# A hybrid decoder layer on one core: GpSimd's sums, dots, folds and three weight remainders on VectorE, and gate products placed behind their operands

## The chip, the core and the metric

The kernel runs on one core of one Trainium2 chip. A core has five engines that run their own queues in order and wait for each other through semaphores: TensorE (PE: matmuls from on-chip memory, SBUF, into the accumulation memory, PSUM), VectorE (DVE: elementwise work and scans), ScalarE (ACT: activation functions, casts, copies), GpSimd (POOL: elementwise work, and transfers that it issues itself) and SyncE (SP: here it only issues transfers). PEld is TensorE's loading of stationary operands. The metric is the time of one execution in microseconds of device time; lower is better. A profile is one execution with every instruction recorded.

## The reference

One layer, batch 1, 1024 tokens, 1024 channels. All arithmetic is to float32 accuracy.

```python
mod = silu(c) @ mod_w + mod_b
shift, scale, gate = split(mod, 3)
h = rmsnorm(x, norm_g) * (1 + scale) + shift
cv, cg, cs, lx, ls = split(h @ w_in, 5)              # 1024 columns each

v = causal_depthwise_conv(cv * sigmoid(cg), dw_w, dw_b)      # 31 taps
v = silu(layernorm(v, cln_g, cln_b))                         # over channels
y_conv = (v @ pw2_w + pw2_b) * silu(cs)

xs = causal_depthwise_conv(lx, sc_w, sc_b)                   # 4 taps
r = sigmoid(xs @ wr + br); i = sigmoid(xs @ wi + bi)         # by heads of 128
a = exp(-8 * r * softplus(-lam))
hs = linear_scan(a, sqrt(1 - a*a) * i * xs)                  # h_t = a_t h_{t-1} + b_t
y_lru = hs * silu(ls)

x = x + (1 + gate) * (concat(y_conv, y_lru) @ w_out)
out = rmsnorm(x, final_g)
```

## The kernel before

Everything is held transposed: channels on the 128 partitions, tokens along the free axis, so a tensor of 1024 channels is eight tiles of 128x1024. A float32 product is made of three reduced-precision ones: each operand is split into a high part (a cast, on ScalarE) and a remainder (full minus high, a subtraction of two SBUF tiles), and high x high, high x remainder and remainder x high are accumulated. The suffixes `hi` and `lo` (weights), `h` and `l` (inputs) name these parts.

**The slots.** The 40 output tiles of `w_in` and the eight of the LRU half of `w_out` are worked off one after the other; each is a slot with a number `n` (0 to 47) and takes 48 matmuls of 128x512: eight input tiles, two halves of the tokens, three products. Slots 0 to 6 are a start group. `ORDER` (line 35) lists the others: `i25` is output tile 25 of `w_in`, `g1` stands for the gate products of LRU head 1. `weights` (468) prepares a slot's weights: a transfer into `raw`, a cast to `whi` on ScalarE, and the remainder `wlo` on GpSimd for slots below `EARLY` and on VectorE from there on. `raw`, `whi` and `wlo` have two buffers each. Slots 4 to 13 have theirs on GpSimd before.

**The LRU half.** When a slot of `lx` is done, `evac_in` (1112) reads it from PSUM: two activations on ScalarE, six tap accumulations on VectorE make `xs`; `split` makes `xsh` on ScalarE and `xsl` (`xs` minus `xsh`, VectorE). `gates` (1156) then has 12 matmuls of 128x512: the gate weights' high part with `xsh`, the same with `xsl`, their remainder with `xsh`. Sigmoids, exponential, tangent and square root follow on ScalarE, products and the scan on VectorE, and at last `yh` and `yl`, the inputs of the LRU half of `w_out` (slots 40 to 47).

**The convolution.** `conv_tile` (1003) has 31 taps for each of the eight tiles of `v`. Five tiles are accumulated tap by tap on VectorE; the three in `POOLED` (1, 3, 5) by ScalarE, which writes scaled copies `cq` and `co`, and by transfers that GpSimd issues and that add them into `es` and `oo` (`conv_pooled`, 1054). At the end of a pooled tile, `last` (1082) folds `es` and `oo` into the tile `c` with three instructions on the engine `FOLD`. `conv_sum` (1090) adds up the eight finished tiles in the order `SUMS`: seven additions of 128x1024, six on GpSimd and the last on VectorE. All but the last may start only when the first matmul of slot `CSUM` has started (`after`). The layer norm (1196) takes the mean from that sum, by one product with ones (`mean`, line 1202). Its result goes through the pointwise product (`pw2`), while PE works on the LRU half of `w_out`.

**The gate modulation.** `gate_mod` (1186) is called in slots 14 to 21 (`GM`). It loads 128 rows of `mod_w` into `modw` through SP and calls `dot` (794), which multiplies them with the activated `c` (in `sc`) and sums along the row. Where `GDOT` is `'POOL'`, GpSimd makes the product and ScalarE sums it in an activation with an accumulator; where it is `'DVE'`, VectorE does both in one instruction. The sixteen dots of shift and scale at the start already run on VectorE.

**The order.** All instructions go first into a `Plan` (102). `order` (159) simulates the engines with costs for every operation and writes each engine's queue in the planned order; the chip then runs the queues in this order, with waits on real data. A free engine takes the ready operation with the lowest `prio`: a slot's work has about its number, the convolution has 1000 and more, so it fills what is left. `ready` is the planned end of what an operation needs, plus a latency (line 201). The planner lets VectorE and GpSimd wait for each other where both work on SBUF alone (`lock`, `held`).

Of the kernel before, what the change touches and what calls it, by code (L numbers as in the profile page):

```python
# [12 lines left out]
ALU = mybir.AluOpType  # L13
# [34 lines left out]
TLATE = 2  # L48
QGATES = ((2, 5), (3, 0), (3, 2), (3, 2))
PEARLY = (3,)  # L50
CSUM = 36
OUT_A, OUT_P, OUT_Z = (6,), (0, 1, 2), (7,)
KORD = (0, 1, 2, 3, 4, 5, 6, 7)
WPW = ("DVE", "DVE", "DVE", "DVE")
# [12 lines left out]
SPP = 25  # L67
PAD = 16
GLO = 'DVE'
GDOT = 'POOL'  # L70
FOLD = 'POOL'
EARLY = 14
ISSUE, FLIGHT, RATE = 1.0, 10.0, 3.0
GM = 14
TAPP = 15
# [20 lines left out]

class Op:
    __slots__ = ("eng", "cost", "emit", "prio", "table", "bufs", "succ", "wait", "ready",
                 "seq", "reserve", "columns", "lock", "end", "psum", "lag")


class Plan:
# [21 lines left out]
                    yield (it, i)  # L124

    def op(self, eng, cost, emit, prio, r=(), w=(), table=None, after=(), reserve=0,
           columns=0, lock=False, lag=0.0):
        o = Op()
        o.lag = lag
        o.eng, o.cost, o.emit, o.prio, o.table = eng, cost, emit, prio, table  # L130
        o.succ, o.ready, o.seq, o.reserve = [], 0.0, len(self.ops), reserve
        o.columns = columns
        o.lock = not lag and eng == "POOL" or eng == "DVE" and lock
        r, w = list(self.keys(r)), list(self.keys(w))
        preds = set(after)
        for k in r:
            if k in self.writer:
                preds.add(self.writer[k])
        for k in w:
            if k in self.writer:  # L140
                preds.add(self.writer[k])
            preds.update(self.readers.get(k, ()))
        for k in r:
            self.readers.setdefault(k, []).append(o)
        for k in w:
            self.writer[k] = o
            self.readers[k] = []
        preds.discard(o)
        o.wait = len(preds)
        for p in preds:  # L150
            p.succ.append(o)
        o.bufs = list(dict.fromkeys(k[0] for k in r + w if isinstance(k[0], Buf)))
        for b in o.bufs:
            b.left += 1
        o.psum = [(b, any(k[0] is b for k in w)) for b in o.bufs if b.pool == "bank"]
        self.ops.append(o)
        return o

    def order(self):
        free = {p: cap for p, (_, _, _, cap) in self.pools.items()}  # L160
        live = set()
        engines = ("PE", "ACT", "DVE", "POOL", "SP")
        until = {"PE": 1.0, "ACT": 2.5, "DVE": 2.6, "POOL": 1.1, "SP": SP0}
        pending = {e: [] for e in engines}
        for o in self.ops:
            if o.wait == 0:
                pending[o.eng].append(o)
        releases, out, table, t, ticks = [], [], "silu", 0.0, {0: self.BUSY}
        held = {"DVE": 0.0, "POOL": 0.0}
        waiting = None  # L170
        left = len(self.ops)

        def clear(o):

            return max((e + self.LATENCY[g] for b, w in o.psum
                        for d in ((b.read, b.written) if w else (b.written,))
                        for g, e in d.items() if g != o.eng), default=0.0)

        def done(o, end):
            until[o.eng] = end  # L180
            if o.lag:
                self.pipe = max(self.pipe, end) + o.lag
                end = max(self.pipe, end + FLIGHT)
            elif o.eng == "SP":
                self.pipe = end = max(self.pipe, end - o.cost) + o.cost
                until["SP"] = max(end - o.cost + 0.4, end - BACKLOG)
            o.end = end
            for b, w in o.psum:
                (b.written if w else b.read)[o.eng] = end
            for b in o.bufs:  # L190
                b.left -= 1
                if b.left == 0 and b.pool in free:
                    heapq.heappush(releases, (end, b.name, b.pool))
            for s in o.succ:
                lat = 0.0 if o.eng == "PE" and s.eng == "PE" else \
                    0.11 if o.eng == s.eng == "DVE" else self.LATENCY[o.eng]
                if o.eng == "SP" and o.prio > 0:
                    lat = LANDING if o.prio < 37 else 3.0
                if s.prio >= 1000 and s.eng != o.eng and o.prio < 2000:
                    lat += MARGIN  # L200
                s.ready = max(s.ready, end + lat)
                s.wait -= 1
                if s.wait == 0:
                    pending[s.eng].append(s)

        while left:
            while releases and releases[0][0] <= t:
                free[heapq.heappop(releases)[2]] += 1
            moved, later = False, []
            if waiting and held["DVE"] <= t + 1e-9:  # L210
                o, waiting, moved = waiting, None, True
                held["POOL"] = t + o.cost
                done(o, t + o.cost)
            for e in engines:
                if until[e] > t + 1e-9:
                    continue
                best, key = None, None
                for o in pending[e]:
                    if o.ready > t + 1e-9:
                        continue  # L220
                    if e == "DVE" and o.lock and held["POOL"] > t + 1e-9:
                        later.append(held["POOL"])
                        continue
                    k = (o.prio + (2.0 if o.table and o.table != table else 0.0), o.seq)
                    if key is not None and k >= key:
                        continue
                    need = {}
                    for b in o.bufs:
                        if b.pool in free and b not in live:
                            need[b.pool] = need.get(b.pool, o.reserve * (b.pool == "big")) + 1  # L230
                    if any(free[p] < n for p, n in need.items()):
                        continue
                    if o.psum and clear(o) > t + 1e-9:
                        later.append(clear(o))
                        continue
                    best, key = o, k
                if best is None:
                    continue
                o, moved = best, True
                pending[e].remove(o)  # L240
                left -= 1
                cost = o.cost
                if o.table and o.table != table:
                    cost, table = cost + self.SWITCH, o.table
                if e == "PE":
                    if t < self.COLD or ticks.get(int(t / self.TICK) - 1, 0) < self.BUSY:
                        cost *= 2
                    i = int((t + cost) / self.TICK)
                    ticks[i] = ticks.get(i, 0) + o.columns
                end = t + cost  # L250
                out.append((t, o))
                for b in o.bufs:
                    if b.pool in free and b not in live:
                        live.add(b)
                        free[b.pool] -= 1
                if e == "POOL" and o.lock and held["DVE"] > t + 1e-9:
                    waiting, until[e] = o, float("inf")
                    continue
                if o.lock:
                    if e == "DVE":  # L260
                        end = max(t, held["POOL"]) + cost
                    held[e] = end
                done(o, end)
            if not moved:
                nxt = later + [u for u in until.values() if t + 1e-9 < u < float("inf")]
                nxt += [o.ready for e in engines for o in pending[e] if o.ready > t + 1e-9]
                if releases:
                    nxt.append(releases[0][0])
                assert nxt, "no operation can go on"
                t = min(nxt)  # L270
        return out
# [11 lines left out]
def hymba_layer(ctx: ExitStack, tc: tile.TileContext, xT, vecs, mod_w, w_first, w_in,  # L283
# [806 lines left out]
    def conv_sum():  # L1090
        for i in SUMS[1:]:
            a, end = c[SUMS[0]] if i == SUMS[1] else csum, i == SUMS[-1]
            TT(1000 + 5 * i, "DVE" if end else "POOL", csum, a, c[i], ALU.add, r=[a, c[i]],
               w=[csum], after=[] if end else [started[CSUM]])


# [59 lines left out]
    def gates(i, n):  # L1156
# [3 lines left out]
        for j, (dst, b) in enumerate(((r, "br"), (g, "bi"))):  # L1160
            ps = Two(f"gate{i}_{j}")
            for c0, c1 in FULL:
                def emit(j=j, ps=part(ps, c0, c1), c0=c0, c1=c1):
                    for lhs, rhs, st in ((hi, xh, 0), (hi, xl, 1), (lo, xh, 2)):
                        pe.matmul(ps(), lhs()[:, j, :], rhs()[:, c0:c1], start=st == 0,
                                  stop=st == 2)
                S.op("PE", 3 * 0.2267, emit, n + 0.01 * j, [hi, lo, xh, xl], halves(ps, c0, c1),
                     columns=3 * H)
                ACT(n + 0.2, part(dst, c0, c1), part(ps, c0, c1), AF.Sigmoid, H, bias=vec(b, i),
                    r=halves(ps, c0, c1), w=[dst])  # L1170
        pr = n + 1.0
# [314 lines left out]
```

## Time and profile before

| | us |
|---|---|
| three runs | 753.58, 750.99, 749.26 |
| median | 750.99 |
| the profiled execution, its time | 752.39 |
| the profiled execution, its span from first to last instruction | 750.5 |

The busy times of the engines and the stretches that matter are shown where the prediction uses them. In rows of instructions, `out<-in` are tile names of the program; a time in brackets at the end is the idle time of the engine ahead of that instruction, with what ended it. `L480` are the slots' matmuls, `L1165` the gate products, `L352` a tensor-tensor operation of VectorE or GpSimd, `L344` a scalar-tensor-tensor operation of VectorE, `L333` and `L325` ScalarE's activations and casts. Matmuls overlap, so the distance between two starts, not the duration of one, is what a matmul costs.

PE's work in order: the start group to about 85 us, the slots of `w_in` with the gate products to 481.85 us, the LRU half of `w_out` to 574 us, `pw2` to 651 us, the convolution half of `w_out` to 740 us, and the last stores.

### The profile page before, as it was taken

The numbers are of one execution on the slowest core, as the hardware profiler recorded it, in microseconds if no ns is written. First come the engines' busy times: TensorE is split into PE (matmuls) and PEld (weight loads), VectorE is DVE, ScalarE is ACT, GpSimd is POOL, SyncE is SP. The second block draws the span as 40 slices with busy tenths as digits, with TensorE's granted clock in tenths as the row PEclk, the third lists the DMA queues.
The fourth block names the chain that finished last, engine by engine and source line by source line (L and its number), as shares of the span: only waits on it lengthen the run. The fifth ranks groups of instructions, "written<-read, shape, count | busy, mean of one in ns | idle before, by whom it ended". The sixth has DMA issues, their size and how long they took to land. (4 is left out here: it accounts for less than half of the span.)

```text
span 750.5 us, 8997 instructions
## 1 busy us (share of the span) xinstructions
PE 732.9 (98%) x3314; PEld 608.0 (81%) x3314; DVE 619.9 (83%) x858; ACT 466.0 (62%) x627; POOL 162.0 (22%) x137
## 2 busy tenths in 40 slices
PE   9999999999999999999999899999999999999994
PEld 8888888887888888888888688878888888878884
DVE  6999999999799881788899995839799857998544
ACT  7660697677978977855959486714584334656331
POOL 0033023363163331532113343020000000000003
PEclk9999999999999999999999899999999999999998
DMA  9961034686699799598383436643224330534006
GB/s 338 408 210 50 0 117 102 154 182 155 173 220 221 144 216 218 123 216 176 103 177 73 108 69 195 168 166 143 99 98 155 116 123 17 208 113 141 28 1 224
DMA packets 37052, 111.59 MB, mean 149 GB/s; under 512 B 4112, under 2 KB 12816, under 8 KB 37008
## 3 DMA queue, kind: packets, MB, share of 16 engines
q1 hardware_dynamic: 23616, 75.97, 29.0%
q0 software_dynamic: 12528, 34.26, 25.2%
q10 hardware_dynamic: 864, 0.79, 0.3%
q8 instruction: 26, 0.43, 0.2%
q14 instruction: 18, 0.15, 0.1%
HBM read 64.16 MB, written 12.58 MB: 102 GB/s over the span
## 5 line engine op out<-in xcount | busy, mean ns | idle before, releaser
L480 PE MATMUL ps<-uh,whi 128*128 128x512 f32 x576 | 224.6, 390 | 0.0
L480 PE MATMUL ps<-ul,whi 128*128 128x512 f32 x576 | 224.5, 390 | 0.0
L480 PE MATMUL ps<-uh,wlo 128*128 128x512 f32 x576 | 224.4, 390 | 0.0
L480 PEld LDWEIGHTS ps<-uh,whi 128*128 128x128 f32 x576 | 108.5, 188 | 22.6
L480 PEld LDWEIGHTS ps<-ul,whi 128*128 128x128 f32 x576 | 108.3, 188 | 22.5
L480 PEld LDWEIGHTS ps<-uh,wlo 128*128 128x128 f32 x576 | 108.3, 188 | 22.4
L325 ACT CAST whi<-raw 128x1024 fp32r<-128x1024 f32 x46 | 48.1, 1048 | 58.5 <-PE ps L480 42.5
L357 POOL DMA_DIRECT2D es<-cq x45 | 41.4, 920 | 141.2 <-ACT cq L333 101.3
L333 ACT ACT_TABLE_LOAD x48 | 61.6, 1283 | 11.8 <-DVE c L352 5.2
L352 DVE TENSOR_TENSOR wlo<-raw,whi 128x1024 fp32r<-128x1024 f32 x36 | 46.2, 1283 | 18.5 <-ACT whi L325 18.0
L352 POOL TENSOR_TENSOR o<-fin,bc 128x256 f32<-128x256 f32 (+1 forms) x8 | 7.2, 940 | 236.6 <-ACT bc L325 236.6
L344 DVE SCALAR_TENSOR_TENSOR cacc<-v,V,cacc 128x511 f32<-128x511 f32 (+14 forms) x75 | 55.8, 744 | 0.4
L344 DVE SCALAR_TENSOR_TENSOR caccs<-v,V,caccs 128x511 f32<-128x511 f32 (+6 forms) x70 | 52.2, 746 | 1.3
L344 DVE SCALAR_TENSOR_TENSOR caccs<-c,wsum,caccs 128x511 f32<-128x511 f32 (+6 forms) x70 | 52.0, 743 | 0.5
L480 PE MATMUL ps<-yh,whi 128*128 128x512 f32 x128 | 50.5, 394 | 0.0
L480 PE MATMUL ps<-yh,wlo 128*128 128x512 f32 x128 | 49.9, 390 | 0.0
L480 PE MATMUL ps<-yl,whi 128*128 128x512 f32 x128 | 49.8, 389 | 0.0
L357 POOL DMA_DIRECT2D oo<-co x42 | 41.3, 1012 | 36.0 <-ACT co L333 17.5
L352 POOL TENSOR_TENSOR wlo<-raw,whi 128x1024 fp32r<-128x1024 f32 x10 | 24.9, 2503 | 111.0 <-ACT whi L325 111.0
L344 DVE SCALAR_TENSOR_TENSOR xs<-ps,V,xs 128x512 f32<-128x512 f32 (+3 forms) x48 | 35.8, 746 | 3.0 <-ACT xs L333 2.9
L333 ACT ACTIVATE cq<-v,V 128x511 f32<-128x511 f32 (+14 forms) x45 | 31.8, 709 | 0.3 <-DVE r L1178 0.3
L333 ACT ACTIVATE cq<-c,wsum 128x512 f32<-128x512 f32 x42 | 29.8, 713 | 0.0
(338 smaller groups left out, 1518.7 us busy)
## 6 DMA issues: line engine op xcount, KB each, us to landing
raw<-in_w_in_dram SPq DMA_DIRECT2D x36, 512.0 KB, 4.7
modw<-in_mod_w_dram SPq DMA_DIRECT2D x24, 512.0 KB, 9.2
raw<-in_w_out_dram SPq DMA_DIRECT2D x10, 512.0 KB, 3.5
x<-in_xT_dram SPq DMA_DIRECT2D x8, 512.0 KB, 10.7
scsd<-scs SPq DMA_DIRECT2D x8, 512.0 KB, 3.9
acc<-in_xT_dram SPq DMA_DIRECT2D x8, 512.0 KB, 4.3
accd<-acc SPq DMA_DIRECT2D x8, 512.0 KB, 2.7
rawpw<-in_pw_dram SPq DMA_DIRECT2D x8, 512.0 KB, 3.4
```

What stands on the lines that cost most here:

```text
L325: act.copy(out(), in_())
L333: act.activation(out=out(), in_=in_(), func=func, **kw)
L344: dve.scalar_tensor_tensor(out=out(), in0=in0(), scalar=scalar, in1=in1(), op0=op0, op1=op1, accum_out=accum)
L352: lambda: e.tensor_tensor(out=out(), in0=a(), in1=b(), op=op), prio, r, w,
L357: return S.op("POOL", ISSUE, lambda: pool.dma_start(out(), a(), accum_op=ALU.add), prio, r, w, lag=RATE * n / T, after=after)
L480: pe.matmul(part(ps, a - off, b - off)(), k3(lhs)()[:, k, :], rhs[k]()[:, a:b], start=(k == 0 and lhs is wh and rhs is xh and (a - off) % ...
```

## The change

Three choices of engine move from GpSimd to VectorE, for the dots of the gate modulation, for the folds of the pooled convolution tiles, and for the first six sums over the convolution tiles. The remainders of slots 11 to 13 move from GpSimd to VectorE as well. The sums may start from slot 38 on instead of slot 36. And operations have a new property, `slack`, which the planner adds to an operation's readiness after predecessors on other engines; the gate products get 5 us of it. It changes the planned order and adds no wait on the chip.

```diff
-CSUM = 36
+CSUM = 38
+GSLACK = 5.0
+SUMENG = "DVE"
...
-GDOT = 'POOL'
-FOLD = 'POOL'
-EARLY = 14
+GDOT = 'DVE'
+FOLD = 'DVE'
+EARLY = 11
...
-        o.lag = lag
+        o.lag, o.slack = lag, slack
...
+                if s.eng != o.eng:
+                    lat += s.slack
                 s.ready = max(s.ready, end + lat)
...
-            TT(1000 + 5 * i, "DVE" if end else "POOL", csum, a, c[i], ALU.add, r=[a, c[i]],
+            TT(1000 + 5 * i, "DVE" if end else SUMENG, csum, a, c[i], ALU.add, r=[a, c[i]],
                w=[csum], after=[] if end else [started[CSUM]])
...
                 S.op("PE", 3 * 0.2267, emit, n + 0.01 * j, [hi, lo, xh, xl], halves(ps, c0, c1),
-                     columns=3 * H)
+                     columns=3 * H, slack=GSLACK)
```

More of the change, by code (lines that the diff above doesn't have):

```diff
@@ L98 @@
     __slots__ = ("eng", "cost", "emit", "prio", "table", "bufs", "succ", "wait", "ready",
-                 "seq", "reserve", "columns", "lock", "end", "psum", "lag")
+                 "seq", "reserve", "columns", "lock", "end", "psum", "lag", "slack")
 class Plan:
@@ L126, in op @@
     def op(self, eng, cost, emit, prio, r=(), w=(), table=None, after=(), reserve=0,
-           columns=0, lock=False, lag=0.0):
+           columns=0, lock=False, lag=0.0, slack=0.0):
         o = Op()
-        o.lag = lag
+        o.lag, o.slack = lag, slack
         o.eng, o.cost, o.emit, o.prio, o.table = eng, cost, emit, prio, table
```

## The prediction

> **What bounds the kernel now.** First the page's head and its busy times, to see which engine sets the end.
>
> ```profile
> span 750.5 us, 8997 instructions
> PE 732.9 (98%) x3314; PEld 608.0 (81%) x3314; DVE 619.9 (83%) x858; ACT 466.0 (62%) x627; POOL 162.0 (22%) x137
> ```
>
> PE is busy 98% of the span, so only two things shorten the kernel: fewer gaps on PE, or matmuls that follow each other faster. Busy time hides the second, so I read the view of stretches of 20 us, where the number in brackets after a busy time counts instructions; after the five engines stands the granted clock.
>
> ```profile
> 160.00:180.00 20.00, 18.25 (x81) 14.80 (x80) 19.96 (x25) 13.95 (x19) 9.18 (x7) 1.00 0.95 209
> 400.00:420.00 20.00, 20.00 (x90) 16.58 (x89) 20.00 (x23) 17.07 (x22) 6.29 (x6) 1.00 0.53 104
> 420.00:440.00 20.00, 16.68 (x62) 13.18 (x61) 17.92 (x22) 11.66 (x14) 2.87 (x1) 0.83 0.10 30
> ```
>
> An undisturbed stretch carries 90 matmuls. Two fall short: 160 to 180 us with 81, and 420 to 440 us with 62 at a clock of 0.83. The view of PE's waits says on what:
>
> ```profile
> PE gate L1165 <- DVE xsl L352: 5.1, 2, 3.3
> PE pbout L590 <- DVE l34out L352: 1.1, 1, 1.1
> ```
>
> Both waits of the gate products are for `xsl`, the remainder of the LRU input that VectorE computes. PE in order of time gives their price (first column the start, then the duration):
>
> ```profile
> 173.45 0.39 PE L1165 MATMUL gate<-xsh,ghi 128*128 128x512 f32 x1
> 175.59 0.50 PE L1165 MATMUL gate<-xsl,ghi 128*128 128x512 f32 x1 [1.75 <-DVE xsl L352]
> ...
> 420.30 0.39 PE L1165 MATMUL gate<-xsh,ghi 128*128 128x512 f32 x1
> 424.00 0.79 PE L1165 MATMUL gate<-xsl,ghi 128*128 128x512 f32 x1 [3.31 <-DVE xsl L352]
> ...
> 430.13 0.40 PE L480 MATMUL ps<-uh,whi 128*128 128x512 f32 x1
> 430.36 0.39 PE L480 MATMUL ps<-ul,whi 128*128 128x512 f32 x1
> ```
>
> Undisturbed starts lie 0.23 us apart (430.13 to 430.36). The first stall costs 175.59 - 173.45 - 0.23 = 1.9 us. The second costs 424.00 - 420.30 - 0.23 = 3.5 us, and afterwards PE is slow: from 424.00 to 430.13 there are 14 steps in 6.13 us where 14 x 0.23 = 3.2 would do, so 2.9 us more. Together 8.3 us.
>
> Why is `xsl` late? VectorE and GpSimd at these two places, and the view of the tile (min/median/max in ns):
>
> ```profile
> 171.66 3.87 DVE L352 TENSOR_TENSOR xsl<-xs,xsh 128x1024 fp32r<-128x1024 f32 x1
> 417.24 3.43 DVE L352 TENSOR_TENSOR wlo<-raw,whi 128x1024 fp32r<-128x1024 f32 x1
> 421.25 2.70 DVE L352 TENSOR_TENSOR xsl<-xs,xsh 128x1024 fp32r<-128x1024 f32 x1
> ```
>
> ```profile
> 171.74 2.70 POOL L352 TENSOR_TENSOR modw<-modw,sc 128x1024 f32<-128x1024 f32 x1
> 416.82 2.75 POOL L352 TENSOR_TENSOR csum<-c,c 128x1024 f32<-128x1024 f32 x1
> 419.65 3.21 POOL L352 TENSOR_TENSOR csum<-csum,c 128x1024 f32<-128x1024 f32 x1
> ```
>
> ```profile
> L352 DVE TENSOR_TENSOR xsl<-xs,xsh x8: 1220/1228/3874, 113.2 to 453.0; 128x1024 fp32r<-128x1024 f32 x8
> ```
>
> An `xsl` takes 1.23 us as a rule and 3.87 or 2.70 when GpSimd works on a 128x1024 tensor at the same time. The one of 171.66 ends at 175.53, 1.09 us after GpSimd's dot ends at 174.44: it did next to nothing before. The remainder of 417.24 ends at 420.67, 1.1 us after the first sum (419.57). So the two stalls are a gate-modulation dot (`GDOT`) and the sum over the conv tiles (`SUMENG`) on GpSimd, holding up VectorE just ahead of a gate product. [...]
>
> **The change, part by part.** What leaves GpSimd:
>
> ```profile
> L352 POOL TENSOR_TENSOR wlo<-raw,whi 128x1024 fp32r<-128x1024 f32 x10 | 24.9, 2503 | 111.0 <-ACT whi L325 111.0
> L352 POOL TENSOR_TENSOR modw<-modw,sc 128x1024 f32<-128x1024 f32 x8 | 22.2, 2771 | 13.6 <-DMA modw<-in_mod_w_dram 13.6
> ```
>
> The groups that show VectorE's price of the same work, from the groups by shape, then the accumulator reads and the sum by tile:
>
> ```profile
> L352 DVE TENSOR_TENSOR wlo<-raw,whi 128x1024 fp32r<-128x1024 f32 x36 | 46.2, 1283 | 18.5 <-ACT whi L325 18.0
> L344 DVE SCALAR_TENSOR_TENSOR modw<-modw,sc 128x1024 f32<-128x1024 f32 x15 | 18.3, 1223 | 0.0
> L352 DVE TENSOR_TENSOR c<-c,caccs 128x512 f32<-128x512 f32 x5 | 3.4, 685 | 0.0
> ```
>
> ```profile
> L344 DVE DVE_READ_ACCUMULATOR modw<-modw,sc x15: 77/85/97, 11.4 to 68.6; 128x1 f32 x15
> ```
>
> ```profile
> L352 POOL TENSOR_TENSOR csum<-csum,c x5: 2706/3214/4267, 419.7 to 451.0; 128x1024 f32<-128x1024 f32 x5
> L1202 PE MATMUL mean<-csum,ones_d x4: 590/592/592, 505.0 to 506.3; 128*128 128x512 f32 x4
> L352 DVE TENSOR_TENSOR csum<-csum,c x1: 1217/1217/1217, 499.0 to 499.0; 128x1024 f32<-128x1024 f32 x1
> ```
>
> - `EARLY` 14 to 11: the remainders of slots 11, 12, 13 (three of the ten on GpSimd; seven stay). VectorE gets 3 x 1.28 = 3.8 us.
> - `GDOT`: eight products leave GpSimd, and the eight accumulating passes of ScalarE go with them; VectorE does each in one instruction and an accumulator read, 8 x (1.22 + 0.085) = 10.5 us.
> - `FOLD`: three tiles x three folds of 128x512, 9 x 0.69 = 6.2 us.
> - `SUMENG`: six of the seven sums, 6 x 1.22 = 7.3 us; `CSUM` lets five of them start two slots later.
>
> VectorE gets 27.8 us more. Is there room? Two long stretches, VectorE in the third pair of numbers:
>
> ```profile
> 60.00:180.00 120.00, 118.25 (x529) 97.90 (x528) 117.16 (x197) 77.21 (x107) 35.75 (x27) 1.00 0.46 107
> 180.00:480.00 300.00, 296.69 (x1296) 245.15 (x1295) 244.32 (x288) 229.53 (x306) 103.40 (x89) 0.99 0.71 159
> ```
>
> Until 180 us it is full (117.16 of 120), and the three remainders fall there; they push back convolution taps, which carry the last priority. SP's load of the weights two slots on waits for each remainder (`raw` has two buffers); 1.28 us instead of 2.50 releases it no later unless VectorE's queue does. From 180 to 480 us it idles 55.7 us, enough for all 27.8. It also gets time back: at the two stalls alone (3.87 - 1.23) + (3.43 - 1.28) + (2.70 - 1.23) = 6.3 us. Behind the moved sums waits the layer norm: its last sum ends at 500.2 us and PE's mean starts at 505.0, so 4.8 us of lateness are covered; without that cover each microsecond shows once the LRU output products, which fill PE meanwhile, run out. I cost the 27.8 us at nothing on the path.
>
> A new wait: the dot now waits on VectorE for its weights' transfer. On GpSimd that was
>
> ```profile
> POOL modw L352 <- DMA modw<-in_mod_w_dram: 13.6, 2, 7.8
> ```
>
> The transfers themselves stay on SP's queue. Behind the waiting dot now stand evacuations and `xsl`, and PE behind these. The low bound is nothing, if the transfers are there by the planned time; the high one is both waits in full less 5 us of distance each, 13.6 - 10 = 3.6 us. I take 0.5, near the low end: GpSimd arrived early because it had little to do, VectorE has a queue.
>
> - `GSLACK`: no instruction; the planner counts a gate product ready 5 us after its operands from other engines, and fills PE with the next product's steps meanwhile. Its cover is the next product; its cost is a later gate chain (second rival). Gain: it hides lateness of `xsl` up to 5 us, and the worst seen was 3.3 us of idle.
>
> Either part alone would end the stalls, so I count the 8.3 us once and whole. Bounds: at the least the first stall's 1.9 us, if a new wait replaces the other; at most 8.3 plus the 1.1 us wait of `pbout`.
>
> **Sum.** Span 750.5 - 8.3 + 0.5 = 742.7 us; the profiled execution took 752.39, so 744.6 of its kind; the median of the runs shown, 750.99, lies 1.4 lower. Forecast: 743.2, rounded to 743.
>
> **Rivals.**
> 1. *VectorE waits for the dots' transfers*, up to the 3.6 us instead of 0.5: 743 + 3.1 = 746. For it: VectorE executes in order, and two of eight transfers were late. Against: 5 us of distance at the gates.
> 2. *The last gate comes too late.* Five microseconds on the last gate push the LRU outputs:
>
> ```profile
> 457.37 0.39 PE L1165 MATMUL gate<-xsh,ghi 128*128 128x512 f32 x1
> ```
>
> ```profile
> 478.49 8.03 DVE L352 TENSOR_TENSOR yl<-sls,yh 128x1024 fp32r<-128x1024 f32 x7
> ```
>
> ```profile
> 481.85 0.39 PE L480 MATMUL ps<-yh,whi 128*128 128x512 f32 x1
> ```
>
> The last `yl` is done at 486.52; PE needs it 7 x 3 x 0.227 = 4.8 us after 481.85, at 486.6. Spare 0.1 us, so up to 4.9 us of idle plus 2.9 us of slow clock as at 424: 743 + 7.8 = 751, no change. Against: the sums, the last begun at 451.0, no longer slow VectorE ahead of this gate, and PE can take the second half's first seven steps.
> 3. *VectorE becomes the bound (slower).* If the added work does not find the idle time, the convolution's end and the layer norm slip; PE runs out of LRU products. It decides from 4.8 + 7.8 = 12.6 us of slip (cover plus net gain). Taken whole less what the collisions give back: 27.8 - 6.3 - 4.8 = 16.7 us, 743 + 16.7 = 760. For it: 117.16 of 120 us before 180. Against: the 55.7 us after. [...]
> 4. *The stalls are this execution's own*, and the timed runs hold others: 751.
>
> **How the numbers follow.** Chances: forecast 0.60, rival one 0.18, two 0.08, three 0.10, four 0.04. Half a per cent is 3.75 us (about what a measurement can tell from no change), so faster is below 747.2: the forecast and two thirds of rival one, 0.72. Same: the rest of rival one, two and four, 0.18. Slower: 0.10. Range: below, the 743 less the 1.1 us of `pbout` and the 1.7 by which the fastest run lies under the median, 740; above, up to 750, short of rival two, with rival three left out.
>
> **What would show it.** Right: no `gate` row among PE's waits; no `xsl` over 1.3 us; 90 matmuls and clock 1.00 in the stretches around 170 and 430 us; 26 fewer instructions on GpSimd; VectorE near 640 us busy. Wrong: PE waiting for `yl` near 480 us or for layer-norm operands near 570 us, or VectorE idle for `modw` longer than 5 us at once.

## The result, and the profile after

Both kernels ran twelve times in one comparison. Before: median 750.69 us (747.77 to 753.58). Changed: median 744.65 us (743.41 to 746.89). The ratio is 0.9921, with a 95% interval of 0.9906 to 0.9936: 6.0 us, or 0.8%, are gone. The profiled execution of the changed kernel took 744.65 us, its span was 742.9.

The head and the busy times of the page after:

```profile
span 742.9 us, 8983 instructions
PE 728.2 (98%) x3314; PEld 604.9 (81%) x3314; DVE 628.4 (85%) x892; ACT 458.0 (62%) x611; POOL 102.0 (14%) x111
```

GpSimd has 137 - 111 = 26 instructions fewer. VectorE has 34 more (26 moved, eight accumulator reads), yet only 628.4 - 619.9 = 8.5 us more of busy time. PE is as busy as before, so again the gaps and the clock must be read. Lines of the changed kernel stand four higher: L484 for L480, L1169 for L1165, L356 for L352, L348 for L344, L329 for L325.

PE's waits after (what waited, for whom, us in all, times, the longest):

```profile
PE first L755 <- ACT fhi L329: 1.9, 1, 1.9
PE pbout L594 <- DVE l34out L356: 1.1, 1, 1.1
```

There is no `gate` row any more. The stretches, with VectorE in the third pair of numbers and the clock after the five engines:

```profile
160.00:180.00 20.00, 20.00 (x90) 16.57 (x89) 20.00 (x30) 13.28 (x18) 5.21 (x6) 1.00 0.65 162
420.00:440.00 20.00, 20.00 (x90) 16.58 (x89) 19.61 (x26) 16.20 (x19) 1.74 (x2) 1.00 0.35 86
60.00:180.00 120.00, 120.00 (x538) 99.66 (x537) 117.33 (x200) 75.56 (x103) 23.40 (x23) 1.00 0.43 107
180.00:480.00 300.00, 300.00 (x1326) 248.48 (x1325) 260.51 (x327) 228.15 (x300) 61.10 (x71) 1.00 0.74 165
```

The two stretches that had 81 and 62 matmuls have 90 each, and the clock near 430 us is 1.00 instead of 0.83. From 60 to 480 us PE has no gap at all. The tile that was late (min/median/max in ns):

```profile
L356 DVE TENSOR_TENSOR xsl<-xs,xsh x8: 1200/1220/1225, 114.2 to 442.3; 128x1024 fp32r<-128x1024 f32 x8
```

No `xsl` is stretched now; the worst was 3.87 us and is 1.23.

The span shrank by 7.6 us, while the stalls of the first profile were worth 8.3. Most of the difference is at the start: a product at the end of the start group begins 1.0 us later than before. The same instruction in the timelines of before, and after:

```profile
83.47 1.62 PE L930 MATMUL psbias<-ones,fsum 128*128 128x1 f32 x14
```

```profile
84.45 1.62 PE L934 MATMUL psbias<-ones,fsum 128*128 128x1 f32 x14
```

PE executes the same instructions in the same order in both kernels up to 114 us, and in the fourteen profiles of this study this product begins between 83.28 and 84.45 us; with the moves alone it is 83.64. So the difference is taken as the execution's and not the change's, though no second profile of the changed kernel settles it. The 1.9 us wait of `first` for ScalarE in the list above need not be its cause: in the kernel with the dots alone that wait is 1.0 us, and the product begins at 83.30. The rest, 0.3 us, was not followed.

### The profile page after: what moved, and what is told of

It is laid out like the page before. It is cut to its first block, busy times and chain, and to the rows that moved or that the text cites. A ratio compares the mean times of both kernels' runs of the same rounds, so it can differ in the third digit from the quotient of the medians.

```text
span 742.9 us, 8983 instructions
## 1 busy us (share of the span) xinstructions
PE 728.2 (98%) x3314; PEld 604.9 (81%) x3314; DVE 628.4 (85%) x892; ACT 458.0 (62%) x611; POOL 102.0 (14%) x111
## 4 chain that ended last, share of the span: by engine, by line
PE 89%; DVE 7%; DMA 1%; issue 1%; ACT 1%; SPq 0%; DVEq 0%
PE ps L484 64%; PE first L755 5%; PE gate L1169 3%; PE puout L594 2%; PE pupw L594 2%; PE pbpw L594 2%; PE papw L594 2%; PE paout L594 1%; PE pbout L594 1%; PE out L660 1%; DMA fraw<-in_w_first_dram 1%; DVE o L348 1%; PE pcout L594 1%; PE late L755 1%; PE pcpw L594 1%
## 5 line engine op out<-in xcount | busy, mean ns | idle before, releaser
L484 PE MATMUL ps<-uh,whi 128*128 128x512 f32 x576 | 224.2, 389 | 0.0
L484 PE MATMUL ps<-ul,whi 128*128 128x512 f32 x576 | 224.1, 389 | 0.0
L484 PE MATMUL ps<-uh,wlo 128*128 128x512 f32 x576 | 224.1, 389 | 0.0
L484 PEld LDWEIGHTS ps<-uh,whi 128*128 128x128 f32 x576 | 108.2, 188 | 22.5
L484 PEld LDWEIGHTS ps<-uh,wlo 128*128 128x128 f32 x576 | 108.1, 188 | 22.5
L484 PEld LDWEIGHTS ps<-ul,whi 128*128 128x128 f32 x576 | 108.1, 188 | 22.3
L329 ACT CAST whi<-raw 128x1024 fp32r<-128x1024 f32 x46 | 48.1, 1049 | 36.8 <-PE ps L484 33.4
L361 POOL DMA_DIRECT2D es<-cq x45 | 39.6, 895 | 183.1 <-ACT cq L337 159.0
L356 DVE TENSOR_TENSOR wlo<-raw,whi 128x1024 fp32r<-128x1024 f32 x39 | 47.6, 1220 | 16.7 <-ACT whi L329 16.7
L348 DVE SCALAR_TENSOR_TENSOR cacc<-v,V,cacc 128x511 f32<-128x511 f32 (+14 forms) x75 | 55.7, 743 | 0.2
L348 DVE SCALAR_TENSOR_TENSOR caccs<-v,V,caccs 128x511 f32<-128x511 f32 (+6 forms) x70 | 52.1, 745 | 1.2
L348 DVE SCALAR_TENSOR_TENSOR caccs<-c,wsum,caccs 128x511 f32<-128x511 f32 (+6 forms) x70 | 52.1, 744 | 0.2
L484 PE MATMUL ps<-yh,whi 128*128 128x512 f32 x128 | 50.4, 394 | 0.0
L484 PE MATMUL ps<-yh,wlo 128*128 128x512 f32 x128 | 49.8, 389 | 0.0
L484 PE MATMUL ps<-yl,whi 128*128 128x512 f32 x128 | 49.8, 389 | 0.0
L356 POOL TENSOR_TENSOR o<-fin,bc 128x256 f32<-128x256 f32 (+1 forms) x8 | 7.2, 931 | 288.3 <-ACT bc L329 288.3
L348 DVE SCALAR_TENSOR_TENSOR xs<-ps,V,xs 128x512 f32<-128x512 f32 (+3 forms) x48 | 35.8, 745 | 0.1
L356 POOL TENSOR_TENSOR wlo<-raw,whi 128x1024 fp32r<-128x1024 f32 x7 | 17.7, 2542 | 88.9 <-ACT whi L329 88.9
```

Of the source, the lines that this page charges most:

```text
L329: act.copy(out(), in_())
L348: dve.scalar_tensor_tensor(out=out(), in0=in0(), scalar=scalar, in1=in1(), op0=op0, op1=op1, accum_out=accum)
L356: lambda: e.tensor_tensor(out=out(), in0=a(), in1=b(), op=op), prio, r, w,
L361: return S.op("POOL", ISSUE, lambda: pool.dma_start(out(), a(), accum_op=ALU.add), prio, r, w, lag=RATE * n / T, after=after)
L484: pe.matmul(part(ps, a - off, b - off)(), k3(lhs)()[:, k, :], rhs[k]()[:, a:b], start=(k == 0 and lhs is wh and rhs is xh and (a - off) % ...
```

## The experiments

Theory A is that of the prediction: GpSimd's work on 128x1024 tensors holds up VectorE just ahead of a gate product, and taking away either the collision (the moves) or its consequence (the distance of 5 us) ends the stalls. Theory B: the distance shields the gate products only, so a collision left in place finds another operand that PE needs. Theory C: the added work on VectorE costs something that the gain hides. All diffs are against the changed kernel.

### Each half alone

```diff
# distance alone
-CSUM = 38
-SUMENG = "DVE"
-GDOT = 'DVE'
-FOLD = 'DVE'
-EARLY = 11
+CSUM = 36
+SUMENG = "POOL"
+GDOT = 'POOL'
+FOLD = 'POOL'
+EARLY = 14
```

> Only the 5 us of distance ahead of the gate products; all sums, dots, folds and remainders on GpSimd as before. Theory A (the prediction: either half of the change ends both stalls): no gate row among PE's waits, although single xsl still take 2.5 to 4 us; span about 743 us, ratio to the kernel before 0.990 to 0.994. Theory B (the collisions on VectorE cost PE elsewhere as well, so the moves are needed): the gate waits go, but other waits of PE for VectorE or a stretch with fewer than 88 matmuls stay; span 746 to 750 us, ratio 0.995 to 1.000.

Measured: median 746.17 us (743.36 to 749.32, ten runs) beside 750.29 of the kernel before in the same comparison; ratio 0.9941 [0.9923, 0.996]; span 744.9. The gate products do not wait. But another product does, as the timeline of this kernel shows (start, duration, engine; the bracket is the idle time ahead, with what ended it):

```profile
436.54 6.01 POOL L356 TENSOR_TENSOR csum<-csum,c 128x1024 f32<-128x1024 f32 x2
437.29 3.02 DVE L356 TENSOR_TENSOR wlo<-raw,whi 128x1024 fp32r<-128x1024 f32 x1
...
440.23 3.41 DVE L356 TENSOR_TENSOR xsl<-xs,xsh 128x1024 fp32r<-128x1024 f32 x1
...
440.36 0.50 PE L484 MATMUL ps<-uh,wlo 128*128 128x512 f32 x1 [1.91 <-DVE wlo L356]
```

Two sums on GpSimd stretch a weight remainder to 3.02 us and then an `xsl` to 3.41. The `xsl` is hidden, since its gate comes later. The remainder has no such distance, and PE waits 1.9 us for it. By its mechanism this is theory B; the ratio, 0.9941, lies between the ranges of the two theories. The runs spread over 6 us, against 3.5 of the changed kernel.

```diff
# moves alone
-GSLACK = 5.0
+GSLACK = 0.0
```

> All moves to VectorE as in the changed kernel, distance 0. Theory A: no xsl over 1.3 us, so it is there when planned; no gate wait; span about 743 us, ratio 0.990 to 0.994. Theory C (VectorE runs late against the plan even without collisions, because it is full until 180 us, so the distance is what counts): one or two gate waits of 1 to 3 us stay, with or without the slow clock behind them; span 745 to 750 us, ratio 0.993 to 1.000.

Measured: 744.57 us (743.85 to 744.81, five runs), ratio 0.9921 [0.9909, 0.9933], span 742.1, no gate wait. The tile view of this kernel:

```profile
L356 DVE TENSOR_TENSOR xsl<-xs,xsh x8: 1218/1226/1246, 113.4 to 440.3; 128x1024 fp32r<-128x1024 f32 x8
```

The moves alone do all of it. Once nothing stretches `xsl`, 5 us of distance cover nothing.

### One move undone, with the distance kept

```diff
# sums back on GpSimd
-CSUM = 38
-SUMENG = "DVE"
+CSUM = 36
+SUMENG = "POOL"
```

> The changed kernel with the six sums back on GpSimd and their start at slot 36; distance of 5 us kept. Theory A: some VectorE instructions of 128x1024 take 2.5 to 4.5 us between 410 and 460 us again, but the distance hides them from PE: no gate wait, span within 1 us of the changed kernel (742 to 744 us), ratio 0.990 to 0.994. Theory B: the sums delay a gate product or the last LRU chain by more than 5 us: span 746 us or more.

```diff
# dots back on GpSimd
-GDOT = 'DVE'
+GDOT = 'POOL'
```

> The changed kernel with the eight gate-modulation dots back on GpSimd and ScalarE; distance kept. Theory A: xsl of 2.5 to 4 us return between 150 and 250 us, hidden by the distance: span 742 to 744 us, ratio 0.990 to 0.994. Theory B: VectorE's lateness shows on PE between 150 and 250 us as a wait of 1 us or more: span 744 to 747 us.

Measured: 744.43 us (five runs; 0.9923 [0.991, 0.9936]) with the sums back, 744.40 us (five runs; 0.9922 [0.9909, 0.9936]) with the dots back. In each the collision is there, in the tile's maximum. First the kernel with the sums back, then the one with the dots back:

```profile
L356 DVE TENSOR_TENSOR xsl<-xs,xsh x8: 1221/1226/3746, 114.2 to 439.1; 128x1024 fp32r<-128x1024 f32 x8
```

```profile
L356 DVE TENSOR_TENSOR xsl<-xs,xsh x8: 1204/1226/3016, 113.9 to 441.3; 128x1024 fp32r<-128x1024 f32 x8
```

One `xsl` takes 3.75 or 3.02 us, and PE does not wait for it. The stretched one and its gate product in the two timelines, in the same order:

```profile
439.09 3.75 DVE L356 TENSOR_TENSOR xsl<-xs,xsh 128x1024 fp32r<-128x1024 f32 x1
...
449.83 0.39 PE L1169 MATMUL gate<-xsh,ghi 128*128 128x512 f32 x1
```

```profile
172.33 3.02 DVE L356 TENSOR_TENSOR xsl<-xs,xsh 128x1024 fp32r<-128x1024 f32 x1
...
178.91 0.39 PE L1169 MATMUL gate<-xsh,ghi 128*128 128x512 f32 x1
```

Only the second shows the distance at work. With the moves alone, where the distance is zero, the gate products of heads 0, 1, 5 and 6 start 0.5 to 0.7 us after their `xsl` ends, those of the other four 7.5 to 10.8 us after it. The `xsl` of 172.33 is that of head 1, and without the distance it would have come too late. The one of 439.09 is that of head 7, which has 7.5 us of room without any distance. So the dots show that the distance shields a gate product, the sums do not; and in the profile of the distance alone PE waited only for what is not a gate product.

### One move alone, with no distance

```diff
# sums alone
-GSLACK = 5.0
-GDOT = 'DVE'
-FOLD = 'DVE'
-EARLY = 11
+GSLACK = 0.0
+GDOT = 'POOL'
+FOLD = 'POOL'
+EARLY = 14
```

> From the kernel before, only the six sums go to VectorE (start at slot 38); dots, folds and remainders stay on GpSimd, no distance. If each stall belongs to its own GpSimd work: the second stall (3.5 us and 2.9 us of slow clock) is gone, a gate wait of 1 to 2 us behind a dot near 175 us stays; span 750.5 - 6.4 = 744 us, ratio 0.991 to 0.995. If the stalls come from the planned order as a whole, both go or both stay.

```diff
# dots alone
-CSUM = 38
-GSLACK = 5.0
-SUMENG = "DVE"
-FOLD = 'DVE'
-EARLY = 11
+CSUM = 36
+GSLACK = 0.0
+SUMENG = "POOL"
+FOLD = 'POOL'
+EARLY = 14
```

> From the kernel before, only the eight dots go to VectorE and their accumulating passes leave ScalarE; no distance. If each stall belongs to its own GpSimd work: no gate wait near 175 us, the wait near 420 us with its slow clock stays; span 750.5 - 1.9 = 748.6 us, ratio 0.996 to 0.999. If the order as a whole decides: anything between 743 and 752 us.

Measured, beside 751.67 us of the kernel before (13 runs): sums alone 744.13 us (four runs; 0.9905 [0.988, 0.993]; span 741.9), dots alone 745.95 us (four runs; 0.9927 [0.9902, 0.9952]; span 743.5). Neither went as expected.

With the sums alone the stall near 172 us should have stayed, since the dots are on GpSimd as before. It is not there. The timeline of this kernel:

```profile
171.90 3.49 POOL L356 TENSOR_TENSOR modw<-modw,sc 128x1024 f32<-128x1024 f32 x1 [0.49 <-DMA modw<-in_mod_w_dram]
171.91 1.22 DVE L356 TENSOR_TENSOR xsl<-xs,xsh 128x1024 fp32r<-128x1024 f32 x1
...
173.70 2.78 DVE L356 TENSOR_TENSOR wlo<-raw,whi 128x1024 fp32r<-128x1024 f32 x1
```

Dot and `xsl` meet as in the profile of before, but this time `xsl` runs through in 1.22 us, the dot takes 3.49, and the next VectorE instruction, a remainder with time to spare, is the one held up. Whether PE loses 1.9 us here is settled by which of the two goes through first.

With the dots alone the stall of 6.4 us near 420 us should have stayed. PE's waits and its timeline in this kernel:

```profile
PE gate L1169 <- DVE xsl L356: 1.5, 1, 1.5
```

```profile
418.08 0.39 PE L1169 MATMUL gate<-xsh,ghi 128*128 128x512 f32 x1
419.95 0.50 PE L1169 MATMUL gate<-xsl,ghi 128*128 128x512 f32 x1 [1.48 <-DVE xsl L356]
```

It is 419.95 - 418.08 - 0.23 = 1.6 us, and no slow matmuls follow. The remainder that the first sum had stretched now slips in ahead of it, so only one of two collisions hits. Moving the dots changes the planned order around the sums as well; which single placement did it was not separated. The intervals of the two ratios overlap, but both hold the spread of the kernel before; the runs themselves do not (743.74 to 744.72 us with the sums, 745.31 to 746.25 with the dots, four each). So the sums alone are some 1.8 us better than the dots alone, in line with the wait that is left.

### Folds and remainders

```diff
# folds and remainders back on GpSimd
-FOLD = 'DVE'
-EARLY = 11
+FOLD = 'POOL'
+EARLY = 14
```

> The changed kernel with the folds and the remainders of slots 11 to 13 back on GpSimd: the two parts for which no stall was found. If they carry nothing: span 742 to 744 us, ratio 0.990 to 0.995, as the changed kernel. If the folds or remainders matter: a wait of PE for wlo between 120 and 160 us or for layer-norm operands near 570 us, span over 746 us.

Measured: 744.31 us (four runs; 0.9923 [0.9898, 0.9949]), span 741.7, no gate wait. Beside the 744.65 of the changed kernel these two edits carry nothing that the runs can tell.

### The distance that is too long, and VectorE as the bound

```diff
# rival two provoked
-GSLACK = 5.0
+GSLACK = 15.0
```

> The changed kernel with the distance tripled to 15 us, to try the second rival (the last gate product comes too late for the LRU products of the output). The last gate moves from 449.8 us to about 453 to 459 us. If that rival's mechanism holds: PE waits for yl near 475 us by up to 8 us, with slow clock behind it; ratio to the kernel before 0.994 to 1.005. If the planner covers it with other steps: no wait, span 742 to 744 us, ratio 0.990 to 0.994.

Measured: 744.95 us (four runs; 0.991 [0.9879, 0.994]), span 743.2. The gate products now start 15 to 16 us behind their `xsl`, and the last one comes at 453.8 us, against 457.4 before:

```profile
453.82 0.39 PE L1169 MATMUL gate<-xsh,ghi 128*128 128x512 f32 x1
```

PE has no wait for `yl`. Three times the distance does not bring about rival two.

```diff
# rival three provoked: convolution tile 5 on VectorE too
-POOLED = (1, 3, 5)
+POOLED = (1, 3)
```

> The changed kernel with convolution tile 5 accumulated on VectorE in place of ScalarE and transfers: some 45 instructions of 0.74 us, 33 us more on VectorE, more than the change itself moved; a test of the third rival (VectorE as the bound). If VectorE's idle time of about 40 us between 180 and 480 us takes it up: the layer norm's mean moves from 482.5 us by less than 10 us and the span stays within 2 us of the changed kernel, ratio 0.990 to 0.996. If VectorE is the bound: the mean slips by more than 20 us, PE waits for layer-norm operands after 540 us, span 750 us or more, ratio 1.000 or more.

Measured: 748.57 us (746.71 to 751.11, ten runs; 0.9965 [0.9947, 0.9983]), span 744.9: 0.44 percentage points of the ratio, 3.3 us, behind the changed kernel. VectorE is busy for 655.3 us instead of 628.4. The layer norm's mean in the tile view of the sum, in the changed kernel and in this one:

```profile
L1206 PE MATMUL mean<-csum,ones_d x4: 590/592/592, 482.5 to 483.8; 128*128 128x512 f32 x4
```

```profile
L1206 PE MATMUL mean<-csum,ones_d x4: 590/592/592, 503.1 to 504.4; 128*128 128x512 f32 x4
```

It slips by 20.6 us, and only then PE has new waits, in the pointwise product behind the LRU half. PE's waits, then the stretch there:

```profile
PE pupw L594 <- DVE vlc L356: 1.4, 1, 1.4
...
PE pbpw L594 <- ACT epw L329: 0.7, 1, 0.7
...
PE pbpw L594 <- DVE vla L356: 0.2, 1, 0.2
```

```profile
560.00:580.00 20.00, 17.69 (x75) 13.40 (x74) 20.00 (x28) 10.24 (x13) 0.00 (x0) 1.00 0.38 131
```

VectorE is full (20.00 of 20), and PE loses 2.3 us. So rival three's mechanism exists, and the change itself stays clear of it. The mean slips as far as the second outcome had it, but the ratio, 0.9965, lies below its range. The profiled execution is the fastest of the ten (746.71 us), so what the longer ones lose beyond these waits is not known.

### The kernel before, profiled a second time

> The kernel before once more, for a second profile of its two stalls. If their sizes are the same in every execution: gate waits of about 1.8 and 3.3 us and a clock of 0.83 in the stretch from 420 to 440 us again, time 752 us. If the first profile was one of the long ones: the second wait is shorter, less of it is followed by slow matmuls, clock 0.992 to 0.994 over the span, time 749 to 751 us.

Measured: 749.19 us, span 747.4, so 3.1 us shorter than in the first profile. PE's wait and timeline at the second place, in this second profile of the kernel before:

```profile
PE gate L1165 <- DVE xsl L352: 3.3, 1, 3.3
```

```profile
418.20 0.39 PE L1165 MATMUL gate<-xsh,ghi 128*128 128x512 f32 x1
421.91 0.79 PE L1165 MATMUL gate<-xsl,ghi 128*128 128x512 f32 x1 [3.32 <-DVE xsl L352]
...
425.43 0.40 PE L1165 MATMUL gate<-xsh,ghi 128*128 128x512 f32 x1
425.66 0.39 PE L1165 MATMUL gate<-xsl,ghi 128*128 128x512 f32 x1
```

One gate wait instead of two. The second wait is not shorter, as was expected, but less of it is followed by slow matmuls. The idle part is 421.91 - 418.20 - 0.23 = 3.5 us as before, but the slow part has 8 steps in 3.52 us instead of 14 in 6.13, so it costs 3.52 - 8 x 0.23 = 1.7 us instead of 2.9. Together 5.2 us, where the first profile had 8.3; the difference, 3.1, is that of the spans. The first place in the same profile:

```profile
171.56 3.53 POOL L352 TENSOR_TENSOR modw<-modw,sc 128x1024 f32<-128x1024 f32 x1 [0.62 <-DMA modw<-in_mod_w_dram]
171.61 1.22 DVE L352 TENSOR_TENSOR xsl<-xs,xsh 128x1024 fp32r<-128x1024 f32 x1
...
173.40 2.78 DVE L352 TENSOR_TENSOR wlo<-raw,whi 128x1024 fp32r<-128x1024 f32 x1
```

The same two instructions of the same kernel meet within 0.1 us in both profiles. In the first the dot went through and `xsl` waited, here `xsl` went through and the dot waited.

### What a microsecond of idle costs PE

```diff
# gate products put nearer to their operands; the second kernel has -5.0
-GSLACK = 5.0
+GSLACK = -2.5
```

> The changed kernel with a distance of -2.5 us: the gate products whose place hangs on their operands (four of eight, heads 0, 1, 5 and 6) are planned ahead of xsl, so that PE waits some 2 us at each, with no collision on VectorE. If waits of this length leave the clock alone: 4 x 2 = 8 us, span 750 to 752 us, clock 1.00 in all stretches between 100 and 640 us. If any wait slows the clock: 4 x (2 + 2.9) = 20 us, span 760 us or more.

> The same with -5 us: waits of some 4.5 us at up to four gate products. If a wait of over about 3 us is followed by some 6 us of slow matmuls (2.9 us lost), as at 424 us in the kernel before: 4 x (4.5 + 2.9) = 30 us, span 765 to 775 us, and stretches with a clock of 0.8. If the slow clock there had another cause: 4 x 4.5 = 18 us, span 758 to 762 us, clock 1.00.

Measured: 747.85 us (span 746.1) and 747.48 us (span 745.6), one run each. Both miss what they were made for. The planner does not place a gate product before it has placed the instructions that make its operands, so both values plan the same gates, and PE's waits have one row alike in both:

```profile
PE gate L1169 <- DVE xsl L356: 2.2, 4, 0.7
```

Four short waits of at most 0.7 us, each followed by matmuls at full pace (0.23 us apart), so they tell nothing of longer ones. What they show is that such waits cost more than their recorded length: counted by the starts of the matmuls, the four waits of 2.2 us in all cost 3.3 us, and against the span of 742.1 us with no distance the spans are 4.0 and 3.5 us longer.

## Why the prediction held, point by point

**The mechanism.** It held. The two `xsl` that were late are not late in the changed kernel, and with moves alone, without the distance, that is so as well. With the distance kept, leaving the sums or the dots on GpSimd brings a stretched `xsl` back (3.75 and 3.02 us). That no `xsl` is stretched with the sums alone moved, though the dots are on GpSimd, is the luck of a near tie (0.01 us).

**The term that was mis-sized: the 8.3 us of the stalls.** The forecast was 743 us, the measured median is 744.65. The stalls were read rightly from the profile of before, but a second profile of the same kernel has 5.2. Two parts vary: whether the first stall happens (1.9 us or nothing) and how long the matmuls stay slow after the second (2.9 or 1.7 us). The measured gain of 6.0 us lies between the two. The prediction took 1.4 us off to get from its execution to the median, which left the whole gain in; taking the gain itself as 5.2 to 8.3 us would have given 742.4 to 745.5 from 750.7. That the timed runs hold the one kind and the other is likely, from their spread of 5.8 us before and 3.5 after, but no trace of theirs shows it.

**"Either part alone would end the stalls".** Half right. The moves alone end them. The distance alone ends the gate products' waits, and in its profile a 1.9 us wait for a weight remainder takes their place; by the times it gains 4.1 us instead of 6.0.

**27.8 us more on VectorE, costed at nothing.** Right on the path, too cautious on the engine. VectorE was expected near 640 us busy and is at 628.4. By the totals 619.9 + 27.8 - 628.4 = 19.3 us came back, not 6.3: VectorE's instructions had been stretched in more places than those two. Two groups of before, and then the same of after (count, busy us, mean ns):

```profile
L1178 DVE TENSOR_TENSOR_SCAN r<-a,xs 128x1024 f32<-128x1024 f32 x8 | 20.4, 2547 | 0.1
...
L352 DVE TENSOR_TENSOR xsl<-xs,xsh 128x1024 fp32r<-128x1024 f32 x8 | 16.1, 2007 | 1.2 <-ACT xsh L325 1.2
```

```profile
L1182 DVE TENSOR_TENSOR_SCAN r<-a,xs 128x1024 f32<-128x1024 f32 x8 | 18.3, 2284 | 0.0
...
L356 DVE TENSOR_TENSOR xsl<-xs,xsh 128x1024 fp32r<-128x1024 f32 x8 | 9.7, 1216 | 1.2 <-ACT xsh L329 1.2
```

`xsl` alone gives back 6.4 us, the scan 2.1. A third `xsl`, at 453.00 us before, had taken 3.36 us without a wait of PE. Not all of the 19.3 is shown to be collisions: instructions back to back overlap in the record (seven `yl` of 1.22 us fill 8.03 us before), so 27.8 us of durations are less than 27.8 us of busy time. A term of that size is better read from the means of the groups than from the two places where PE waited. All six moved sums, not five, wait for slot `CSUM`; no term hangs on that.

**The wait for the dots' transfers.** Costed at 0.5 us with 0 to 3.6 as bounds; in the profile after it is 0. VectorE's waits hold one row for `modw`, at the start and for another operand:

```profile
DVE modw L348 <- PE c_row L725: 2.0, 1, 2.0
```

**The rivals.** One (transfers) did not happen, by that row. Two (the last gate too late) did not happen either, nor at 15 us of distance: the last gate product came earlier and not later, at 449.8 us instead of 457.4, since its `xsl` was done at 443.48 instead of 456.36. With 15 us PE begins the LRU half at 476.22 and by the prediction's arithmetic would need the last `yl` at 476.22 + 4.8 = 481.0; that is done at 481.82, and yet PE does not wait, so it has other steps to do first. Three (VectorE the bound) needs far more work: the mean did not slip but came at 482.5 instead of 505.0 us, and tile 5 on top was needed for 2.3 us of idle on PE. Four (the stalls are one execution's own) was right in part: one of the two stalls was.

**What stays open.** The layer norm's mean comes 22.5 us earlier in the changed kernel, and it is not known why. With the distance alone, where its sums are still on GpSimd, it comes early too, so the planned order has a part in it; how much is the faster sums was not separated. The earlier mean is worth nothing, since PE is busy with LRU products then. Nor was it separated which placement let the stall shrink with the dots alone.

## What to carry to other kernels

When PE waits now and then for one VectorE result whose duration doubles (here an `xsl` of 1.23 us that took 2.70 and 3.87), look at what GpSimd does in the same microseconds; moving GpSimd's 2.5 us instruction to VectorE can cost VectorE much less than the work that it takes over, here 8.5 us of busy time for 27.8 us of work. A distance in the planned order helps the one consumer it is given to, while removing the collision helps all of them: with the distance alone PE waited 1.9 us for a remainder, with the moves alone for neither a remainder nor an `xsl`. And a stall that hangs on a meeting within 0.1 us should be priced from two profiles, since one of them may hold it and the other not.

## What the runs showed of the hardware

**Near 172 us a near tie decides who is held up.** In three profiles the dot and `xsl` near 172 us start 0.01 to 0.08 us apart by the record, and the order of these starts does not tell who goes through: `xsl` at 171.66 was held by a dot at 171.74, and `xsl` at 171.61 was not held by a dot at 171.56. In two more profiles the starts lie farther apart, and the one that starts first goes through: `xsl` at 171.52 ahead of a dot at 172.23 (distance alone), and a dot at 171.86 ahead of `xsl` at 172.33 (dots back). So it is at a sum: the one at 416.43 was ahead of `xsl` at 416.79, which took 3.10 us (dots alone). What tells is who ends first: in the three near ties the VectorE instruction that is held ends 1.09 us after the dot (175.53 after 174.44 in the profile of before; the remainder at 176.18 after the dot at 175.09 in its second profile, and at 176.48 after 175.39 with the sums alone), almost a whole undisturbed duration of 1.22. At the sums it is the same: there the held instruction ends 1.10 us after (a remainder, 420.67 after 419.57, before), 1.08 us after (`xsl`, 419.89 after 418.81, dots alone) and 1.09 us after (`xsl`, 443.64 after 442.55, distance alone).

**Which idle times of PE were followed by slow matmuls.** Recorded idle times of 1.07 us (`pbout`, before and after), 1.48 (dots alone), 1.75 (before), 1.91 (distance alone) and 1.94 (`first`, after) were followed by matmuls at full pace, 0.23 us apart; both of 3.3 us (3.31 and 3.32) were followed by slow ones, 0.43 us apart, for 6.1 us once and 3.5 us once, with a granted clock of 0.83 and 0.91 in the stretch from 420 to 440 us. So in these profiles the change of pace lies between 1.9 and 3.3 us of recorded idle time, and the price of the same idle time varies by more than a microsecond (2.9 and 1.7 us). Counted by the starts, less one step, both idle times are 3.5 us; the recorded 3.3 us count from a matmul's recorded end, 0.39 us after its start, while undisturbed starts lie 0.23 us apart.
